# A transformer block on one core: reordering the products of the first 2048 projection columns

## The chip, the cores and the metric

The kernel runs on one core of one Trainium2 chip. The core has a matrix engine (TensorE: its matmuls are PE in the profile, its weight loads PEld), VectorE (DVE), ScalarE (ACT), GpSimd (POOL) and SyncE (SP), which issues most of the DMA transfers here. The metric is the device time of one execution in microseconds. Before the change it is 437.45 us as the median of three executions (437.12 to 437.57).

## The reference

The program computes one block: modulation of the input by vectors made from a condition c, a token mixer (attention and retention heads), a normalisation, and a feed-forward part. What this case touches is the beginning:

```python
mod = jax.nn.silu(c) @ w_ada[l] + b_ada[l]
sh1, sc1, g1, sh2, sc2, g2 = jnp.split(mod[:, None, :], N_MOD, axis=-1)
h = x * (1.0 + sc1) + sh1          # 256 tokens x 1024
...
proj = h @ w_in                    # the first 2048 columns: mq, mk, mv, rq
```

All inputs are float32. Every large product is made from three products of rounded parts: each operand is split into a high part (float32 rounded to the format the matmul takes, `F32R`) and a low part (the operand less its high part). The result is high x high + high x low + low x high, summed in PSUM.

## The kernel before

Weights go from HBM into `raw` tiles (128 x 2048 float32, 1 MB, four buffers), issued by SP in `load_raw` (L74). For each half of a raw tile, ScalarE makes the high part `whi` (L66) and VectorE the low part `wlo` (L67); later in the kernel the same pair stands in L1028 and L1042. TensorE then multiplies.

The first stage, "A", makes `h @ w_in[:, :2048]`. The contraction of 1024 is cut in eight k-tiles j of 128. The result (256 tokens x 2048 columns) fills all eight PSUM banks: bank `half * 4 + c * 2 + t` holds token half t and 512 columns. So each k-tile has 8 banks x 3 products = 24 matmuls of 128 x 512, with the tokens as the stationary operand.

Before the products of k-tile j, its part of h must exist. An ada tile holds 128 columns of w_ada for the scale and 128 for the shift, transposed, with 1024 elements each. VectorE multiplies these by the row silu(c) and sums them (`ada`, L154, with a read of the accumulator each), and adds the bias column (L171). Then h is formed from x by scale and bias: `hh`, its high part (named A in the profile, L176 on ScalarE; for j = 0 on VectorE, L189), `h32`, the same in full float32 (A7a or A7b, L176 on ScalarE), and `hl` = h32 - hh (L178 on VectorE).

The order of the work is written out by hand in `SEQ`: "a0 W0 P0 a1 W1 P1 a2 W2 P2 a3 W3 P3 X0 Q0 a4 X1 W4 Q1 P4 a5 W5 P5 ...". "a" sums an ada tile, "W" splits a k-tile's weights and makes its h, "P" issues its products. "X" and "Q" are two weight tiles of another projection (winX), whose products reuse banks 0 to 3 after k-tile 3: after P3 ScalarE copies banks 0 to 3 out (L241), four matmuls with zeros open the banks anew (L218), and the winX products follow (mm3, L81 to L83, 128 x 256). There is no scheduler: each engine runs its instructions in the order in which the program issues them.

Each consumed raw tile lets `load_A` issue the next load, in the order of SEQ: ada tile, then x of the k-tile (L120, tile A3a, A3b, A6a or A6b) and its weights. `PIECES` says into how many transfers a load is cut. Transfers on SP use eight semaphores in turn, so that one waits for the eighth before it to have landed.

At the very start SP loads `first` (c, an identity and biases), then ada tile 0 in pieces of 512, 512 and 1024 columns, then x and the weights of k-tile 0 in four pieces of 512 columns, and then the tiles of k-tile 1. Three float32 matmuls on the first piece (L149) keep TensorE busy until k-tile 0's products.

In `products_A`, k-tiles 0 and 1 (`j < CHUNK`, L204) issue for each 512 columns hh x hi, hh x lo and hl x hi, two matmuls each. From k-tile 2 on, each bank gets its three products one behind the other through `mm3` (L81 hh x hi, L82 hh x lo, L83 hl x hi).

Of the kernel before, what the change touches and what calls it, by code (L numbers as in the profile page):

```python
# [9 lines left out]
AF = mybir.ActivationFunctionType  # L10
OP = mybir.AluOpType
# [16 lines left out]
CONST_AT, FIRST = 1, 2  # L28
T0_AT, XN, PRIME = 4, 256, 3
W0, W1, W2 = (4, 5), (6,), (7,)  # L30
PIECES = dict(ada1=[(0, 512, 1024, 2048)] + [2] * 3 + [1] * 4, winA=[4] * 2 + [2] * 2 + [1] * 4, winX=[1] * 2)
CHUNK = 2
BUSY = 3
SEQ = [(s[0], int(s[1])) for s in
# [17 lines left out]
def _body(nc, a, out, pe, act, dve, sp, cst, wts, big, tmp, ps, dram):  # L52
    f = lambda ap: ap.bitcast(F32)

    def bank(i):
        return ps.tile([128, 512], F32, tag=f"P{i}", name=f"P{i}")

    def slot(n, shape, dt=F32):
        return big.tile(shape, dt, tag=f"A{n}", name=f"A{n}")
# [5 lines left out]
    def split(hi, lo, src):  # L65
        act.activation(hi, src, AF.Copy)  # L66
        dve.tensor_tensor(lo, src, f(hi), OP.subtract)  # L67


    def load_raw(src, pieces=1):  # L70
        t = wts.tile([128, 2048], F32, tag="raw", name="raw", bufs=RAW_BUFS)
        cuts = range(0, 2049, 2048 // pieces) if isinstance(pieces, int) else pieces
        for c0, c1 in zip(cuts, cuts[1:]):
            sp.dma_start(t[:, c0:c1], src[:, c0:c1])  # L74
        return t

    def new_hl():
        return [wts.tile([128, 1024], F32R, tag=n, name=n, bufs=HL_BUFS) for n in ("whi", "wlo")]

    def mm3(o, lh, ll, rh, rl, start, stop):  # L80
        pe.matmul(o, lh, rh, start=start, stop=False)  # L81
        pe.matmul(o, lh, rl, start=False, stop=False)  # L82
        pe.matmul(o, ll, rh, start=False, stop=stop)  # L83
# [67 lines left out]
    def ada(raw, sec, j, rows=slice(0, 1024)):  # L151

        junk = tmp.tile([128, 1024], mybir.dt.bfloat16, name="junk", bufs=1)
        dve.tensor_tensor_reduce(out=junk[:, rows], in0=raw[:, rows], in1=srow[:, rows], scale=1.0, scalar=0.0,  # L154
                                 op0=OP.mult, op1=OP.add, accum_out=mod[:, sec, j:j + 1])


    hh = slot(0, [128, 8, 256], F32R)
    hl = slot(1, [128, 8, 256], F32R)
    pa = [bank(i) for i in range(8)]  # L160

    def h1(j, part):

        if part == 0:
            ra = raws.pop(("ada1", j))
            if j == 0:
                ada(ra, 0, 0, slice(0, 512))
                dve.tensor_tensor(bcol[:, 0, 0:1], bcol[:, 0, 0:1], mod[:, 0, 0:1], OP.add)
            for i in range(2):
                ada(ra[:, i * 1024:(i + 1) * 1024], i, j, slice(512 if i == j == 0 else 0, 1024))  # L170
            dve.tensor_tensor(mod[:, 0:2, j], mod[:, 0:2, j], bcol[:, 0:2, j], OP.add)  # L171
            load_A()
        else:
            h32 = slot(("7a", "7b")[j % 2], [128, 256])
            for o in (h32,) if j == 0 else (hh[:, j], h32):
                act.activation(o, raws["xT", j], AF.Identity, scale=mod[:, 0, j:j + 1], bias=mod[:, 1, j:j + 1])  # L176
            raws.pop(("xT", j))
            dve.tensor_tensor(hl[:, j], h32, f(hh[:, j]), OP.subtract)  # L178

    def halves_A(name, j, mid=lambda: None):  # L180
        rw = raws.pop((name, j))
        for half in range(2):
            hi, lo = whl[name, j, half] = new_hl()
            w = 512 if name == "winA" and j < CHUNK else 1024
            mid_at = 512 if 0 < j < CHUNK else 0
            for c in range(0, 1024, w):
                if name == "winA" and j == half == c == 0:

                    dve.tensor_scalar(hh[:, 0], raws["xT", 0], mod[:, 0, 0:1], mod[:, 1, 0:1],  # L189
                                      op0=OP.mult, op1=OP.add)  # L190
                split(hi[:, c:c + w], lo[:, c:c + w], rw[:, half * 1024 + c:half * 1024 + c + w])
                if half == 0 and c == mid_at:
                    mid()
        load_A()

    def products_A(j):
        for half in range(2):
            hi, lo = whl.pop(("winA", j, half))
            for c in range(2):
                if j < CHUNK:  # L200
                    cs = slice(c * 512, (c + 1) * 512)
                    for i, (x, w) in enumerate(((hh, hi), (hh, lo), (hl, hi))):
                        for t in range(2):
                            pe.matmul(pa[half * 4 + c * 2 + t], x[:, j, t * 128:(t + 1) * 128], w[:, cs],  # L204
                                      start=i == j == 0, stop=False)
                    continue
                for t in range(2):
                    mm3(pa[half * 4 + c * 2 + t], hh[:, j, t * 128:(t + 1) * 128],
                        hl[:, j, t * 128:(t + 1) * 128], hi[:, c * 512:(c + 1) * 512],
                        lo[:, c * 512:(c + 1) * 512], j == 0 or j == 4 and half == 0,  # L210
                        j == 7 or j == 3 and half == 0)

    def products_X(u):

# [12 lines left out]
    whl = {}  # L227
    qk = [slot(n, [128, 1024]) for n in ("2a", "2b")]
    ga = slot(12, [128, 8, 256])
    for do, j in SEQ:  # L230
        if do == "a":
            h1(j, 0)
        elif do == "W":
            halves_A("winA", j, lambda: h1(j, 1))
        elif do == "X":
            halves_A("winX", j)
        elif do == "P":
            products_A(j)
            if j == 3:
                for i in range(4):  # L240
                    act.activation(qk[i % 2][:, i // 2 * 512:i // 2 * 512 + 512], pa[i], AF.Copy)  # L241
# [944 lines left out]
```

## Time and profile before

| | us |
|---|---|
| median of three executions | 437.45 |
| the profiled execution, its own time | 437.32 |
| its span in the trace | 435.5 |
| TensorE matmul busy | 422.5 (97%) |
| VectorE busy | 346.1 (79%) |
| ScalarE busy | 241.7 (55%) |

The granted TensorE clock of the profiled execution is 0.997 of full speed. Times in the rows are microseconds from the start of the span, durations as well unless marked ns. A row of the time line has start, duration, engine, line of the program, operation, what it writes and reads, and in brackets how long the engine was idle before it and what ended that. A matmul's duration covers its way through the pipeline: two matmuls that follow each other at full pace start closer together than their durations.

### The profile page before, as it was taken

How to read it: one execution, taken by the hardware profiler on the slowest of the kernel's cores; microseconds unless marked ns; L12 is line 12 of the kernel's file. 1: busy time of each engine (PE TensorE's matmuls, PEld its weight loads, DVE VectorE, ACT ScalarE, POOL GpSimd, SP SyncE). 2: the span in 40 equal slices, each digit the busy share in tenths (PEclk: the TensorE clock that was granted, in tenths of full speed). 3: DMA queues.
4: the chain of work that ended last, by engine and by line, in shares of the span. 5: the costliest groups of instructions: out<-in, count | busy, mean ns of one | idle time of the engine just before them, and what ended most of it. 6: DMA issues, size and time to landing. Idle time of an engine off the chain costs nothing.

```text
span 435.5 us, 6921 instructions
## 1 busy us (share of the span) xinstructions
PE 422.5 (97%) x2738; PEld 379.0 (87%) x2738; DVE 346.1 (79%) x550; ACT 241.7 (55%) x369; POOL 6.7 (2%) x16
## 2 busy tenths in 40 slices
PE   5999999999999999999999999999999999999993
PEld 2768888877788999999989899899999999999882
DVE  4979689979997999697779887798886665577476
ACT  4466578579774477543453995655445545355500
POOL 0000000100000000000000010000000000000000
PEclk9999999999999999999999999999999999999998
DMA  8999887787468778779672079577766784550001
GB/s 263 412 423 355 319 322 292 304 339 250 147 275 299 289 288 298 279 286 316 236 267 108 0 255 401 186 267 257 278 238 251 288 274 160 195 193 2 2 24 72
DMA packets 19696, 105.72 MB, mean 243 GB/s; under 512 B 2512, under 2 KB 4560, under 8 KB 8784
## 3 DMA queue, kind: packets, MB, share of 16 engines
q1 hardware_dynamic: 18288, 100.29, 62.1%
q0 software_dynamic: 1376, 4.99, 3.4%
q8 instruction: 21, 0.34, 0.3%
q14 instruction: 11, 0.09, 0.1%
HBM read 104.22 MB, written 1.06 MB: 242 GB/s over the span
## 4 chain that ended last, share of the span: by engine, by line
PE 92%; DMA 4%; DVE 2%; issue 1%; ACT 0%; SPq 0%; DVEq 0%
PE P L81 28%; PE P L82 28%; PE P L83 28%; DMA raw<-in_strm 3%; DMA A3b<-in_strm 1%; PE P L532 1%; PE P L534 1%; PE P L535 1%; PE P L776 1%; PE P L828 1%; PE P L847 1%; PE P L871 1%; DVE junk L154 1%; DVE wlo L67 0%; PE P L917 0%
## 5 line engine op out<-in xcount | busy, mean ns | idle before, releaser
L1042 DVE TENSOR_TENSOR wlo<-raw,whi 128x1024 fp32r<-128x1024 f32 x118 | 140.4, 1219 | 24.7 <-ACT whi L1028 24.7
L1028 ACT ACTIVATE whi<-raw 128x1024 fp32r<-128x1024 f32 x118 | 120.2, 1051 | 41.3 <-PE P L83 12.4
L83 PE MATMUL P<-whi,A 128*128 128x512 f32 (+1 forms) x212 | 80.3, 379 | 0.0
L81 PE MATMUL P<-whi,A 128*128 128x512 f32 (+1 forms) x168 | 65.4, 389 | 0.1
L82 PE MATMUL P<-wlo,A 128*128 128x512 f32 (+1 forms) x168 | 64.0, 381 | 0.5 <-DVE wlo L67 0.5
L154 DVE CUSTOM_DVE_ANT_0 junk<-raw,srow 128x1024 bf16<-128x1024 f32 (+1 forms) x49 | 58.7, 1197 | 3.5 <-ACT srow L141 1.8
L81 PE MATMUL P<-A3a,whi 128*128 128x256 f32 x192 | 54.4, 283 | 0.0
L81 PE MATMUL P<-A3b,whi 128*128 128x256 f32 x192 | 54.3, 283 | 0.0
L82 PE MATMUL P<-A6b,whi 128*128 128x256 f32 x192 | 54.3, 283 | 0.0
L83 PE MATMUL P<-A3b,wlo 128*128 128x256 f32 x192 | 54.3, 283 | 0.0
L83 PE MATMUL P<-A3a,wlo 128*128 128x256 f32 x192 | 54.3, 283 | 0.0
L82 PE MATMUL P<-A6a,whi 128*128 128x256 f32 x192 | 54.3, 283 | 0.0
L83 PEld LDWEIGHTS P<-whi,A 128*128 128x128 f32 x212 | 39.9, 188 | 7.9
L81 PE MATMUL P<-A,whi 128*128 128x256 f32 x160 | 45.9, 287 | 0.0
L83 PE MATMUL P<-A,wlo 128*128 128x256 f32 x160 | 45.2, 283 | 0.0
L82 PE MATMUL P<-A,whi 128*128 128x256 f32 x160 | 45.2, 283 | 0.0
L81 PEld LDWEIGHTS P<-whi,A 128*128 128x128 f32 x168 | 31.6, 188 | 7.1 <-issue 1.3
L82 PEld LDWEIGHTS P<-wlo,A 128*128 128x128 f32 x168 | 31.7, 188 | 6.7 <-DVE wlo L67 1.2
L82 PEld LDWEIGHTS P<-A6a,whi 128*128 128x128 f32 x192 | 36.8, 192 | 0.3
L81 PEld LDWEIGHTS P<-A3a,whi 128*128 128x128 f32 x192 | 36.8, 192 | 0.3
L81 PEld LDWEIGHTS P<-A3b,whi 128*128 128x128 f32 x192 | 36.9, 192 | 0.0
L82 PEld LDWEIGHTS P<-A6b,whi 128*128 128x128 f32 x192 | 36.9, 192 | 0.0
(235 smaller groups left out, 734.0 us busy)
## 6 DMA issues: line engine op xcount, KB each, us to landing
raw<-in_ada SPq DMA_DIRECT2D x16, 1024.0 KB, 5.2
raw<-in_wup SPq DMA_DIRECT2D x11, 1024.0 KB, 4.8
raw<-in_wgate SPq DMA_DIRECT2D x11, 1024.0 KB, 5.1
raw<-in_wdown SPq DMA_DIRECT2D x11, 1024.0 KB, 4.9
raw<-in_winB SPq DMA_DIRECT2D x10, 1024.0 KB, 5.8
raw<-in_strm SPq DMA_DIRECT2D x8, 1024.0 KB, 6.6
raw<-in_strm SPq DMA_DIRECT2D x11, 512.0 KB, 7.2
raw<-in_winGr SPq DMA_DIRECT2D x4, 1024.0 KB, 6.0
```

The lines of the kernel that those rows point to most:

```text
L81: pe.matmul(o, lh, rh, start=start, stop=False)
L82: pe.matmul(o, lh, rl, start=False, stop=False)
L83: pe.matmul(o, ll, rh, start=False, stop=stop)
L154: dve.tensor_tensor_reduce(out=junk[:, rows], in0=raw[:, rows], in1=srow[:, rows], scale=1.0, scalar=0.0, op0=OP.mult, op1=OP.add, accum_o ...
L532: pe.matmul(p, xl(k)[:, tk], hi[:, c], start=False, stop=k == 7)
L534: pe.matmul(p, xh(k)[:, tk], hi[:, c], start=k == 0, stop=False)
L535: pe.matmul(p, xh(k)[:, tk], lo[:, c], start=False, stop=False)
L776: pe.transpose(p[:, i * 128:(i + 1) * 128], roped[:, which * 512 + i * 128:which * 512 + (i + 1) * 128], ident)
L828: pe.matmul(ps2[e][:, c], qkT[0][s, h // 2, qb * 128:(qb + 1) * 128], qkT[1][s, h // 2, :128 + 128 * qb], start=True, stop=True)
L847: pe.matmul(p[64 * e:64 * e + 64, o], v[:, kb, 64 * (h + e):64 * (h + e) + 64], pT[e][:, c], start=kb == 0, stop=kb == 1)
L1028: act.activation(hi, src, AF.Copy)
L1042: dve.tensor_tensor(lo, src, f(hi), OP.subtract)
```

## The change

Three things are changed, all in stage A.

1. Ada tile 0 is loaded in four pieces of 512 columns (before: 512, 512, 1024). Its sums are made in four steps of 512, scale first, then shift; each first half is added into the bias column by a 128 x 1 add.
2. `h1` has three parts instead of two. Part 1 makes hh alone. It stands ahead of the first `whi` of a k-tile for j = 0 (on VectorE), and behind the first `whi` for the others (for j = 1 behind the first 512 columns; before, behind 1024). Part 2 makes h32 and hl, and stands behind the splits of half 1; for j = 3 and 7 behind those of half 0.
3. `products_A` issues, within a k-tile, all products of hh with both halves of the weights (hi, then lo, per 512 columns for j < 2 and per 1024 for the others), and then all products of hl with hi. For j = 3 and 7 this order is kept within half 0 and then within half 1.

The number of matmuls, of splits and of h activations stays the same. Ada tile 0 takes one more DMA, one more sum with its accumulator read, and one more 128 x 1 add.

```diff
-PIECES = dict(ada1=[(0, 512, 1024, 2048)] + [2] * 3 + [1] * 4, ...
+PIECES = dict(ada1=[4] + [2] * 3 + [1] * 4, ...
...
         if part == 0:
             ra = raws.pop(("ada1", j))
-            if j == 0:
-                ada(ra, 0, 0, slice(0, 512))
-                dve.tensor_tensor(bcol[:, 0, 0:1], bcol[:, 0, 0:1], mod[:, 0, 0:1], OP.add)
             for i in range(2):
-                ada(ra[:, i * 1024:(i + 1) * 1024], i, j, slice(512 if i == j == 0 else 0, 1024))
+                rw, at = ra[:, i * 1024:(i + 1) * 1024], 0 if j else 512
+                if at:
+                    ada(rw, i, j, slice(0, at))
+                    dve.tensor_tensor(bcol[:, i, j:j + 1], bcol[:, i, j:j + 1], mod[:, i, j:j + 1], OP.add)
+                ada(rw, i, j, slice(at, 1024))
             dve.tensor_tensor(mod[:, 0:2, j], mod[:, 0:2, j], bcol[:, 0:2, j], OP.add)
             load_A()
+        elif part == 1:
+            x, m = raws["xT", j], [mod[:, i, j:j + 1] for i in range(2)]
+            if j == 0:
+                dve.tensor_scalar(hh[:, j], x, *m, op0=OP.mult, op1=OP.add)
+            else:
+                act.activation(hh[:, j], x, AF.Identity, scale=m[0], bias=m[1])
         else:
             h32 = slot(("7a", "7b")[j % 2], [128, 256])
-            for o in (h32,) if j == 0 else (hh[:, j], h32):
-                act.activation(o, raws["xT", j], AF.Identity, scale=mod[:, 0, j:j + 1], bias=mod[:, 1, j:j + 1])
-            raws.pop(("xT", j))
+            act.activation(h32, raws.pop(("xT", j)), AF.Identity, scale=mod[:, 0, j:j + 1],
+                           bias=mod[:, 1, j:j + 1])
             dve.tensor_tensor(hl[:, j], h32, f(hh[:, j]), OP.subtract)
...
-            mid_at = 512 if 0 < j < CHUNK else 0
             for c in range(0, 1024, w):
-                if name == "winA" and j == half == c == 0:
-                    dve.tensor_scalar(hh[:, 0], raws["xT", 0], mod[:, 0, 0:1], mod[:, 1, 0:1],
-                                      op0=OP.mult, op1=OP.add)
+                first_ = name == "winA" and half == c == 0
+                if first_ and j == 0:
+                    h1(j, 1)
                 split(hi[:, c:c + w], lo[:, c:c + w], rw[:, half * 1024 + c:half * 1024 + c + w])
-                if half == 0 and c == mid_at:
-                    mid()
+                if first_ and j:
+                    h1(j, 1)
+            if name == "winA" and half == (j % 4 != 3):
+                h1(j, 2)
         load_A()

     def products_A(j):
...
+        ws = [whl.pop(("winA", j, half)) for half in range(2)]
+        parts = [(x, ks, (half,)) for half in range(2) for x, ks in ((hh, 2), (hl, 1))]
+        if j % 4 != 3:
+            parts = [(hh, 2, (0, 1)), (hl, 1, (0, 1))]
+        for x, ks, halves_ in parts:
+            for half in halves_:
+                w = 512 if j < CHUNK else 1024
+                for c0 in range(0, 1024, w):
+                    for k in range(ks):
+                        for c in range(c0, c0 + w, 512):
+                            for t in range(2):
+                                pe.matmul(pa[half * 4 + c // 512 * 2 + t], x[:, j, t * 128:(t + 1) * 128],
+                                          ws[half][k][:, c:c + 512],
+                                          start=ks == 2 and k == 0 and (j == 0 or j == 4 and half == 0),
+                                          stop=ks == 1 and (j == 7 or j == 3 and half == 0))
```

More of the change, by code (lines that the diff above doesn't have):

```diff
@@ L30 @@
 W0, W1, W2 = (4, 5), (6,), (7,)
-PIECES = dict(ada1=[(0, 512, 1024, 2048)] + [2] * 3 + [1] * 4, winA=[4] * 2 + [2] * 2 + [1] * 4, winX=[1] * 2)
+PIECES = dict(ada1=[4] + [2] * 3 + [1] * 4, winA=[4] * 2 + [2] * 2 + [1] * 4, winX=[1] * 2)
 CHUNK = 2
@@ L191, in halves_A @@
                 split(hi[:, c:c + w], lo[:, c:c + w], rw[:, half * 1024 + c:half * 1024 + c + w])
-                if half == 0 and c == mid_at:
-                    mid()
+                if first_ and j:
+                    h1(j, 1)
+            if name == "winA" and half == (j % 4 != 3):
+                h1(j, 2)
         load_A()
     def products_A(j):
[L197 to L211, printed above, removed]
@@ L233, in _body @@
         elif do == "W":
-            halves_A("winA", j, lambda: h1(j, 1))
+            halves_A("winA", j)
         elif do == "X":
```

2 lines of the change are left out of this document (1 added, 1 removed).

## The prediction

> **What bounds the kernel now.** I read the page first (its busy table and its chain), then the waits of TensorE, then the early part of the time line.
>
> ```profile
> span 435.5 us, 6921 instructions
> PE 422.5 (97%) x2738; PEld 379.0 (87%) x2738; DVE 346.1 (79%) x550; ACT 241.7 (55%) x369; POOL 6.7 (2%) x16
> PE 92%; DMA 4%; DVE 2%; issue 1%; ACT 0%; SPq 0%; DVEq 0%
> ```
>
> TensorE is busy 97% of the span and makes 92% of the chain that ended last. The change removes no product. So it can only win time in which TensorE waits, and these are the waits of its two streams (matmul and weight load) that bear on this change (view of the waits: us in total, times, longest):
>
> ```profile
> PE P L204 <- DVE A L189: 1.1, 1, 1.1
> PE P L82 <- DVE wlo L67: 0.5, 2, 0.3
> PE P L204 <- ACT A L176: 0.5, 1, 0.5
> PEld P L82 <- DVE wlo L67: 1.2, 2, 0.7
> ```
>
> All lie in the first 30 us. The matmul waits look small because a matmul that has been issued counts as busy until its pipeline is empty, so I measure losses by start times instead. Time line, TensorE, matmuls of k-tiles 2 and 3 and the first ones of X0 (start, duration, instruction):
>
> ```profile
> 22.20 0.50 PE L81 MATMUL P<-whi,A 128*128 128x512 f32 x1
> 22.97 0.51 PE L82 MATMUL P<-wlo,A 128*128 128x512 f32 x1 [0.27 <-DVE wlo L67]
> 23.32 0.50 PE L83 MATMUL P<-whi,A 128*128 128x512 f32 x1
> 23.65 0.39 PE L81 MATMUL P<-whi,A 128*128 128x512 f32 x1
> ...
> 28.43 0.39 PE L81 MATMUL P<-whi,A 128*128 128x512 f32 x1
> 29.06 0.50 PE L82 MATMUL P<-wlo,A 128*128 128x512 f32 x1 [0.24 <-DVE wlo L67]
> 29.73 0.39 PE L81 MATMUL P<-whi,A 128*128 128x512 f32 x1
> ...
> 35.57 0.39 PE L81 MATMUL P<-A,whi 128*128 128x256 f32 x1
> 35.91 0.27 PE L83 MATMUL P<-A,wlo 128*128 128x256 f32 x1
> ```
>
> K-tile 2 starts at 22.20, its fourth matmul at 23.65, and k-tile 3 (21 matmuls on) at 28.43: (28.43 - 23.65) / 21 = 0.228 us is the undisturbed pace. The first three matmuls took 1.45 us where three at pace take 0.68, because the second matmul needs the weights' low half, which comes last. K-tile 3 repeats it: 28.43 to 29.73 is 1.30. After a stall two matmuls come 0.33 to 0.35 apart before the pace is back (22.97, 23.32, 23.65); I call this the restart, 0.2 us in all. From 35.57 on (X0) no wait of a product is in the list.
>
> **What holds the start of k-tile 2.** ScalarE's rows, and one window row (its last two numbers are the DMA share and GB/s):
>
> ```profile
> 20.60 1.06 ACT L66 ACTIVATE whi<-raw 128x1024 fp32r<-128x1024 f32 x1 [2.75 <-DMA raw<-in_strm]
> 21.57 0.58 ACT L176 ACTIVATE A<-A6a,mod 128x256 fp32r<-128x256 f32 x1
> 22.06 0.59 ACT L176 ACTIVATE A7a<-A6a,mod 128x256 f32<-128x256 f32 x1
> 22.55 1.04 ACT L66 ACTIVATE whi<-raw 128x1024 fp32r<-128x1024 f32 x1
> 27.50 0.60 ACT L176 ACTIVATE A<-A6b,mod 128x256 fp32r<-128x256 f32 x1 [0.50 <-DVE mod L171]
> 29.93 0.60 ACT L241 ACTIVATE A2a<-P 128x512 f32<-128x512 f32 x1 [0.39 <-PE P L83]
> 32.49 2.00 ACT L66 ACTIVATE whi<-raw 128x1024 fp32r<-128x1024 f32 x2
> ```
> ```profile
> 10.00:20.00 10.00, 9.42 (x40) 7.26 (x41) 9.50 (x18) 5.00 (x10) 0.00 (x0) 1.00 1.04 412
> ```
>
> ScalarE waited 2.75 us for k-tile 2's first half of weights, which landed at 20.6; the DMA engines were full (share 1.04, 412 GB/s) since 10 us. Then come 1.06 us of whi and 0.58 of hh, to 22.15, and TensorE starts at 22.20. The change keeps this order (first whi, then hh, for j > 0), so **k-tile 2 starts at 22.20 whatever was won before it**.
>
> **Part 1: the first ada tile in four pieces.** The start, VectorE (its last sum before h, and h itself) and TensorE's first product:
>
> ```profile
> 8.09 1.23 DVE L154 CUSTOM_DVE_ANT_0 junk<-raw,srow 128x1024 bf16<-128x1024 f32 x1 [1.40 <-DMA raw<-in_strm]
> 9.55 0.41 DVE L189 TENSOR_SCALAR A<-A3a,mod 128x256 fp32r<-128x256 f32 x1
> 10.11 0.47 PE L204 MATMUL P<-whi,A 128*128 128x512 f32 x1 [1.13 <-DVE A L189]
> ```
>
> VectorE idles 1.40 us until the 512 KB piece has landed and then sums 1024 columns in 1.23 us. With two pieces the first 512 fall into that idle time and half of 1.23 is left, so h and the first product come about 0.5 us earlier (one more read of the accumulator and one more 128x1 add lie in the idle time too). K-tiles 0 and 1 then start up to 0.5 us earlier, k-tile 1 also because its hh (ScalarE) no longer stands behind two whi pieces. All of it ends in a longer wait for the landing at 20.6. Value on the path: 0.
>
> The price is one more transfer on SP's queue. SP's issues of this tile's three pieces and of the fourth piece of the first weights, and then issue to landing of the first of the one and of the other (256 KB each):
>
> ```profile
> 1.17 1.37 SPq L74 DMA_DIRECT2D raw<-in_strm  x3
> 4.48 1.01 SPq L74 DMA_DIRECT2D raw<-in_strm  x1
> ```
> ```profile
> raw<-in_strm SPq DMA_DIRECT2D x1, 256.0 KB, 3.0
> raw<-in_strm SPq DMA_DIRECT2D x1, 256.0 KB, 6.4
> ```
>
> The later piece takes 6.4 where the first takes 3.0: everything after the start queues behind bytes, so SP's extra issue ((1.37 - 0.42) / 2 = 0.47 us) is covered by that backlog, and with it the loads of x and of the first weights that stand behind it on SP. Upper end: the whole latency of a piece in series, 3.0 less its own 0.64 us of data at 412 GB/s, 2.4 us. Lower end: the pieces run sooner and all landings come some tenths earlier. The same bytes go through full engines, which is nearest to no shift; I take +0.03.
>
> **Part 2: all products of hh first, then hl.** For k-tile 2 the order becomes four hi (0.9 us), four lo, the same for half 1, then eight of hl with hi. VectorE's rows for this stretch:
>
> ```profile
> 21.70 1.23 DVE L67 TENSOR_TENSOR wlo<-raw,whi 128x1024 fp32r<-128x1024 f32 x1 [0.43 <-ACT whi L66]
> 22.84 0.42 DVE L178 TENSOR_TENSOR A<-A7a,A 128x256 fp32r<-128x256 f32 x1
> 23.62 1.22 DVE L67 TENSOR_TENSOR wlo<-raw,whi 128x1024 fp32r<-128x1024 f32 x1 [0.37 <-ACT whi L66]
> 24.77 1.22 DVE L154 CUSTOM_DVE_ANT_0 junk<-raw,srow 128x1024 bf16<-128x1024 f32 x1
> 27.30 0.17 DVE L171 TENSOR_TENSOR mod<-mod,first 128x2 f32<-128x2 f32 x1
> 33.58 1.23 DVE L67 TENSOR_TENSOR wlo<-raw,whi 128x1024 fp32r<-128x1024 f32 x1 [2.78 <-ACT whi L66]
> ```
>
> The low half is ready at 21.70 + 1.23 = 22.93. The first lo product now comes at 22.20 + 0.2 + 4 x 0.228 = 23.3: no stall. ScalarE makes whi of half 1 at 22.06 instead of 22.55 (the h32 activation goes behind it), ready 23.1; its first use is at 24.2. VectorE's lo of half 1 then starts at 23.13 and ends near 24.35; first use 25.1. hl follows by 24.75; first use 26.0. K-tile 2 would end at 22.20 + 0.2 + 24 x 0.228 = 27.87 instead of 28.43.
>
> *What is late next*: k-tile 3's hh, which waits for its two ada sums. They start when VectorE is done with k-tile 2: before at 24.77; now lo at 23.13, next start 1.15 on (23.62 to 24.77), hl at 0.42 less the 0.09 by which VectorE's instructions overlap (22.93 against 22.84): 24.61. That is 0.16 earlier, less a few hundredths for the order of waits: I take 0.14. So mod is done at 27.33, hh runs 27.36 to 27.96, TensorE starts k-tile 3 at 28.00 instead of 28.43: **-0.43**. Inside it the low half (28.9 on VectorE) is needed only after four products, 28.00 + 0.2 + 0.91 = 29.1, and hl and the second half have more room still. The fourth matmul falls at 28.00 + 0.2 + 0.68 = 28.9 instead of 29.73, so a further **-0.40**; together -0.83 at X0, whose first matmul moves from 35.57 to 34.74.
>
> *Does X0 take it?* Its third matmul needs the low half made at 33.58 + 1.23 = 34.81, and would come at 35.91 - 0.83 = 35.08. That low half hangs on whi at 32.49, behind ScalarE's four copies of banks 0 to 3. Bank 0 is now full only after half 0's last product, at 30.4 (before: copy at 29.93). Before, the copies came as TensorE filled the banks; now all four banks are full within 0.7 us and ScalarE can run them at its own pace, 0.49 between two starts by 21.57 and 22.06 with 0.58 busy; at 0.52 they are through at 32.5, as before. Cover left: 0.27.
>
> *Further on* k-tiles 4 to 7 had no stall, so the order there is worth nothing. The smallest lead of a weights' low half after X0 that I find is
>
> ```profile
> 72.31 1.22 DVE L1042 TENSOR_TENSOR wlo<-raw,whi 128x1024 fp32r<-128x1024 f32 x1
> 74.63 0.39 PE L82 MATMUL P<-wlo,A 128*128 128x512 f32 x1
> ```
>
> ready at 73.53, used at 74.63: 1.10 us, more than 0.83. So the win should reach the end.
>
> **Sum.** -0.43 - 0.40 + 0.03 = -0.80 us. The profiled execution took 437.32 us (span 435.5 and 1.8 around it), 0.13 under the median of 437.45. So 436.52 for it and **436.65 as the median**. A change of 0.2% is 0.87 us and is about what a measurement of this kernel tells from no change; the forecast lies just inside it.
>
> **Rivals.**
> *(a) The landings come earlier* (the stream of the first 10 us runs better in four equal pieces). For: VectorE's 1.40 us wait shows the 512 KB piece late. Against: the same bytes. K-tile 2 could start earlier until its mod is the last to come, about 0.3 us before the whi that holds it now. Gain 1.1: 436.35.
> *(b) The copies of banks 0 to 3 are slower than I assume.* For: they now start later, at 30.4. Against: every ScalarE pair above starts 0.49 apart. At 0.69 per copy whi of X0 starts at 33.2, its low half is ready at 35.5, X0's third matmul at 35.6, and the gain is 0.3: 437.15.
> *(c) The other side: the fourth piece delays the whole stream.* All landings up to k-tile 2 come in one order through full engines, so a delay at the head is kept. At the upper end of 2.4 us: -0.80 + 2.4 = +1.6, 439.05. It is slower by more than 0.2% only if k-tile 2's landing comes 1.7 us later, at 22.3. Against it speaks the 6.4 us backlog above, in which a fixed latency is hidden.
> [...]
> *(d) It does nothing*, because TensorE's start of k-tile 2 is DMA-held and k-tile 3's is held by hh: this is right for the starts, but the stalls behind the starts (1.45 and 1.30 us for three matmuls) are plain in the rows.
>
> **How the numbers follow.** Forecast 0.63, own range 436.4 to 436.95; (a) 0.12; (b) and smaller losses like it, (d) among them, 0.17; (c) 0.08. The range 436.2 to 437.3 holds all but (c) and the ends. Faster by over 0.2% (under 436.58) are (a) and somewhat over a third of the forecast's range: 0.36. Slower is (c): 0.08. The rest, 0.56, is within.
>
> **What would show it.** Right: TensorE's first product near 9.65; ScalarE's whi of k-tile 2 still at about 20.6 and the start at 22.2; from there an even 0.228 us pace with no wait for wlo; k-tile 3 at 28.0 after a short wait for hh; X0 near 34.75. Wrong: whi of k-tile 2 at another time than 20.6 by more than 0.3; X0's third matmul waiting for wlo; a new wait between 66 and 80 us, where VectorE is nearly full.

## The result, and the profile after

The changed kernel took 435.8 us as the median of seven executions, the kernel before 437.4 us beside it. The ratio is 0.9968 with a 95% interval of 0.9956 to 0.9979, that is 1.4 us less (0.9 to 1.9). In a second comparison on another chip it was 0.9975 (0.9967 to 0.9984). The forecast of 436.65 us is too high, and the time lies below its range.

The profiled execution of the changed kernel took 436.03 us. From its page the span, the busy table and the chain that ended last:

```profile
span 434.3 us, 6926 instructions
PE 422.7 (97%) x2738; PEld 379.0 (87%) x2738; DVE 346.5 (80%) x553; ACT 240.9 (55%) x369; POOL 6.7 (2%) x16
PE 89%; DMA 5%; DVE 2%; SPq 1%; issue 1%; ACT 1%; DVEq 0%; ACTq 0%
```

The matmuls are the same 2738, with nearly the same busy time (422.5 us before, 422.7 after); what was won is waiting. The last product of the kernel before, and then that of the changed kernel, in the time lines of TensorE:

```profile
427.68 0.28 PE L83 MATMUL P<-whi,A 128*128 128x256 f32 x1
```
```profile
426.48 0.28 PE L83 MATMUL P<-whi,A 128*128 128x256 f32 x1
```

It comes 1.20 us earlier. Where does that arise? TensorE in stage A of the changed kernel (start, us from the first start to the last end of a group, instruction, how many):

```profile
9.08 0.70 PE L216 MATMUL P<-whi,A 128*128 128x512 f32 x2
...
15.16 0.73 PE L216 MATMUL P<-whi,A 128*128 128x512 f32 x2 [0.29 <-ACT A L180]
...
21.32 1.21 PE L216 MATMUL P<-whi,A 128*128 128x512 f32 x4 [0.42 <-ACT A L180]
22.36 1.09 PE L216 MATMUL P<-wlo,A 128*128 128x512 f32 x4
...
28.14 1.07 PE L216 MATMUL P<-wlo,A 128*128 128x512 f32 x4
...
33.73 0.39 PE L81 MATMUL P<-A,whi 128*128 128x256 f32 x1
33.96 0.28 PE L82 MATMUL P<-A,whi 128*128 128x256 f32 x1
34.07 0.27 PE L83 MATMUL P<-A,wlo 128*128 128x256 f32 x1
...
45.34 1.35 PE L216 MATMUL P<-whi,A 128*128 128x512 f32 x4
...
47.45 1.07 PE L216 MATMUL P<-whi,A 128*128 128x512 f32 x4
```

The first product moved from 10.11 to 9.08, the start of k-tile 2 from 22.20 to 21.32, and X0 from 35.57 to 33.73. So 1.84 us are won by X0: 0.88 of it is already there when k-tile 2 starts, and 0.96 comes inside k-tiles 2 and 3. After X0 some is given back: the first eight products of k-tile 4 take 47.45 - 45.34 = 2.11 us where eight at the pace of 0.228 take 1.82. ScalarE shows both the gain and the loss:

```profile
19.71 1.06 ACT L66 ACTIVATE whi<-raw 128x1024 fp32r<-128x1024 f32 x1 [2.55 <-DMA raw<-in_strm]
20.68 0.58 ACT L180 ACTIVATE A<-A6a,mod 128x256 fp32r<-128x256 f32 x1
...
26.45 0.60 ACT L180 ACTIVATE A<-A6b,mod 128x256 fp32r<-128x256 f32 x1 [0.36 <-DVE mod L172]
...
29.48 0.60 ACT L249 ACTIVATE A2a<-P 128x512 f32<-128x512 f32 x1 [0.98 <-PE P L216]
29.97 0.59 ACT L249 ACTIVATE A2b<-P 128x512 f32<-128x512 f32 x1
...
31.40 2.02 ACT L66 ACTIVATE whi<-raw 128x1024 fp32r<-128x1024 f32 x2
...
43.38 2.76 ACT L254 ACTIVATE A<-P 128x512 f32<-128x512 f32 x4 [3.11 <-PE P L83]
...
79.58 1.06 ACT L1036 ACTIVATE whi<-raw 128x1024 fp32r<-128x1024 f32 x1 [3.97 <-DMA raw<-in_winB]
```

K-tile 2's first weights landed at 19.71 instead of 20.60. K-tile 3's hh still waits for its sums, and ends at 26.45 + 0.60 = 27.05. The four copies of the winX result (L254) take 2.76 us, 0.69 each, from 43.38; k-tile 4's first four products need all four banks and cannot be through before 46.1. That is the new stall.

The list of waits of TensorE's weight loads says the same:

```profile
PEld P L216 <- ACT A L180: 2.0, 3, 0.8
PEld P L784 <- ACT A3a L786: 0.5, 1, 0.5
PEld P L216 <- ACT A L254: 0.4, 1, 0.4
```

The third line is the stall at k-tile 4. The second is another loss, near 82 us: a late weight tile of another stage held ScalarE for 3.97 us (the last row above), and copies of PSUM behind it. TensorE's lead over the kernel before is 1.56 us ahead of this place (79.85 and 78.29) and 1.20 behind it (84.25 and 83.05). So with 0.27 and 0.36 us given back, the 1.84 of X0 become the 1.20 at the end. In the second profile of this kernel that wait is missing, and the lead falls only from 1.61 at X0 to 1.34 at the end.

### The profile page after: what moved, and what is told of

The parts are those of the page before. It is cut to its first block, busy times and chain, and to the rows that moved or that the text cites. A ratio compares the mean times of both kernels' runs of the same rounds, so it can differ in the third digit from the quotient of the medians.

```text
span 434.3 us, 6926 instructions
## 1 busy us (share of the span) xinstructions
PE 422.7 (97%) x2738; PEld 379.0 (87%) x2738; DVE 346.5 (80%) x553; ACT 240.9 (55%) x369; POOL 6.7 (2%) x16
## 4 chain that ended last, share of the span: by engine, by line
PE 89%; DMA 5%; DVE 2%; SPq 1%; issue 1%; ACT 1%; DVEq 0%; ACTq 0%
PE P L81 25%; PE P L83 25%; PE P L82 24%; PE P L216 7%; DMA raw<-in_strm 3%; DMA raw<-in_winB 2%; SPq L74 1%; PE P L540 1%; PE P L542 1%; PE P L543 1%; PE P L836 1%; PE P L855 1%; PE P L879 1%; PE P L784 1%; DVE wlo L1050 1%
## 5 line engine op out<-in xcount | busy, mean ns | idle before, releaser
L83 PE MATMUL P<-whi,A 128*128 128x512 f32 (+1 forms) x164 | 61.4, 375 | 0.0
L81 PE MATMUL P<-whi,A 128*128 128x512 f32 (+1 forms) x120 | 46.6, 388 | 0.0
L82 PE MATMUL P<-wlo,A 128*128 128x512 f32 (+1 forms) x120 | 45.0, 375 | 0.0
L83 PEld LDWEIGHTS P<-A3b,wlo 128*128 128x128 f32 x192 | 36.9, 192 | 0.0
L83 PEld LDWEIGHTS P<-A3a,wlo 128*128 128x128 f32 x192 | 36.8, 192 | 0.0
L83 PEld LDWEIGHTS P<-whi,A 128*128 128x128 f32 x164 | 30.9, 188 | 5.7
```

## The experiments

What had to be explained: the start of k-tile 2 moved by 0.88 us, and the prediction had said that it would not move. Two theories were set against each other first. One (letter L): the four pieces make the landings earlier. The other (letter B where the expectations use letters): the new order frees buffers earlier, so that later loads are issued earlier, and the pieces do nothing. No kernel below leaves out any part of the computation. In this table "ratio" is the time over that of the kernel before on the same chip; "rate" is the last number of the row of the stretch from 4 to 8 us; "weights" is the start of ScalarE's first split of k-tile 2, that is the landing.

| kernel | ada tile 0 in columns | median us | ratio (95%) | rate GB/s | weights |
|---|---|---|---|---|---|
| before | 512, 512, 1024 | | 1 | 299 | 20.60 |
| changed | 4 x 512 | 435.8 | 0.9968 (0.9956 to 0.9979) | 352 | 19.71 |
| changed, again | 4 x 512 | 435.82 | 0.9975 (0.9967 to 0.9984) | 328 | 19.89 |
| order_only | 512, 512, 1024 | 436.28 | 0.9984 (0.9975 to 0.9993) | 304 | 19.95 |
| pieces_only | 4 x 512 | 436.34 | 0.9981 (0.9972 to 0.9990) | 357 | 19.24 |
| big_piece | 512, 512, 1024 | 436.75 | 0.9994 (0.9985 to 1.0003) | 292 | 20.28 |
| bank_order_4 | 4 x 512 | 435.51 | 0.9968 (0.9956 to 0.9981) | 336 | 19.90 |
| bank_order_again | 4 x 512 | 435.64 | 0.9969 (0.9959 to 0.9978) | 338 | 20.09 |
| two_in_four | 4 x 512 | 435.78 | 0.9971 (0.9961 to 0.9981) | 356 | 20.05 |
| long_rows | 512, 512, 2 x 64 rows of 1024 | 436.90 | 1.0003 (0.9994 to 1.0012) | 233 | 21.11 |
| two_halves | 1024, 1024 | 435.80 | 0.9974 (0.9966 to 0.9983) | 384 | 18.91 |
| eight | 8 x 256 | 438.22 | 1.0029 (1.0019 to 1.0038) | 245 | 21.96 |
| long_first | 1024, 512, 512 | 435.95 | 0.9967 (0.9955 to 0.9980) | 379 | 19.39 |
| three_alike | 704, 704, 640 | 435.55 | 0.9960 (0.9946 to 0.9974) | 373 | 19.70 |
| plain_halves | 1024, 1024 | 435.35 | 0.9954 (0.9941 to 0.9966) | 375 | 19.36 |
| plain_again | 1024, 1024 | 435.39 | 0.9963 (0.9949 to 0.9977) | 378 | 19.66 |
| busy_one | 1024, 1024 | 435.58 | 0.9969 (0.9958 to 0.9979) | 374 | 19.46 |

The medians come from several chips, so compare the ratios. Rate and landing are those of one execution each. Kernels with the same loads differ in the landing by up to 0.85 us (19.24 to 20.09 with four pieces, 19.95 to 20.60 with the old cut), and the two groups overlap, so the ratios decide; a row shows where time can lie, not what a kernel gains in the mean.

### Order alone, pieces alone

The changed kernel with the loads and sums of ada tile 0 as before:

```diff
-PIECES = dict(ada1=[4] + [2] * 3 + [1] * 4, ...
+PIECES = dict(ada1=[(0, 512, 1024, 2048)] + [2] * 3 + [1] * 4, ...
...
+            if j == 0:
+                ada(ra, 0, 0, slice(0, 512))
+                dve.tensor_tensor(bcol[:, 0, 0:1], bcol[:, 0, 0:1], mod[:, 0, 0:1], OP.add)
             for i in range(2):
-                rw, at = ra[:, i * 1024:(i + 1) * 1024], 0 if j else 512
-                if at:
-                    ada(rw, i, j, slice(0, at))
-                    dve.tensor_tensor(bcol[:, i, j:j + 1], bcol[:, i, j:j + 1], mod[:, i, j:j + 1], OP.add)
-                ada(rw, i, j, slice(at, 1024))
+                ada(ra[:, i * 1024:(i + 1) * 1024], i, j, slice(512 if i == j == 0 else 0, 1024))
```

> The new order of products and of hh, h32 and hl, but ada tile 0 loaded and summed as before (512, 512, 1024 columns). Theory L (the 512 KB piece with 4 KB rows is what makes all early landings late): ScalarE's whi of k-tile 2 stays at 20.6, k-tile 3 starts at 28.0, X0 near 34.75, and the time is 0.7 to 0.9 us below before. Theory B (the new order frees buffers sooner, and so the loads come sooner): whi of k-tile 2 comes at 19.7 here too, X0 near 33.7, and the time is that of the changed kernel, 1.4 to 1.6 below before.

The kernel before with the four pieces and the four sums, in the old order of the products:

```diff
-PIECES = dict(ada1=[(0, 512, 1024, 2048)] + [2] * 3 + [1] * 4, ...
+PIECES = dict(ada1=[4] + [2] * 3 + [1] * 4, ...
...
-            if j == 0:
-                ada(ra, 0, 0, slice(0, 512))
-                dve.tensor_tensor(bcol[:, 0, 0:1], bcol[:, 0, 0:1], mod[:, 0, 0:1], OP.add)
             for i in range(2):
-                ada(ra[:, i * 1024:(i + 1) * 1024], i, j, slice(512 if i == j == 0 else 0, 1024))
+                rw, at = ra[:, i * 1024:(i + 1) * 1024], 0 if j else 512
+                if at:
+                    ada(rw, i, j, slice(0, at))
+                    dve.tensor_tensor(bcol[:, i, j:j + 1], bcol[:, i, j:j + 1], mod[:, i, j:j + 1], OP.add)
+                ada(rw, i, j, slice(at, 1024))
```

> Before, with ada tile 0 loaded in four pieces and summed in four steps; all products and h in the old order. Theory L: whi of k-tile 2 at 19.7, the stalls behind the first products of k-tiles 2 and 3 stay (1.45 and 1.30 us for three matmuls), X0 near 34.7, time 0.7 to 0.9 us below before. Theory B: whi of k-tile 2 at 20.6, X0 at 35.6, no change of time beyond 0.1 us.

With the kernel before at 437.15 us on that chip, the order alone is worth 437.15 x (1 - 0.9984) = 0.70 us (0.3 to 1.1) and the pieces alone 0.83 us (0.4 to 1.2). Their sum, 1.5, is near what the whole change gave (1.4, and 1.1 in its second comparison). So the two parts are about equal, adding up lies within the intervals, and the pieces are not worth nothing. Order alone, in TensorE's time line and ScalarE's:

```profile
21.55 1.20 PE L215 MATMUL P<-whi,A 128*128 128x512 f32 x4 [0.40 <-ACT A L179]
22.59 1.08 PE L215 MATMUL P<-wlo,A 128*128 128x512 f32 x4
...
34.01 0.39 PE L81 MATMUL P<-A,whi 128*128 128x256 f32 x1
```
```profile
19.95 1.06 ACT L66 ACTIVATE whi<-raw 128x1024 fp32r<-128x1024 f32 x1 [2.53 <-DMA raw<-in_strm]
20.92 0.58 ACT L179 ACTIVATE A<-A6a,mod 128x256 fp32r<-128x256 f32 x1
```

and pieces alone, TensorE, ScalarE and the stretch from 4 to 8 us (columns: the stretch, its length, busy time of PE, PEld, DVE, ACT and POOL, granted clock, DMA share, GB/s):

```profile
20.85 0.50 PE L81 MATMUL P<-whi,A 128*128 128x512 f32 x1
...
33.92 0.39 PE L81 MATMUL P<-A,whi 128*128 128x256 f32 x1
```
```profile
19.24 1.06 ACT L66 ACTIVATE whi<-raw 128x1024 fp32r<-128x1024 f32 x1 [2.73 <-DMA raw<-in_strm]
```
```profile
4.00:8.00 4.00, 3.88 (x11) 1.83 (x10) 2.81 (x9) 1.51 (x3) 0.00 (x0) 1.00 1.01 357
```

The same stretch of the kernel before:

```profile
4.00:8.00 4.00, 3.88 (x11) 1.72 (x10) 1.56 (x5) 1.20 (x2) 0.00 (x0) 1.00 0.89 299
```

From the start of k-tile 2 to X0 the kernel before took 35.57 - 22.20 = 13.37 us, order alone takes 34.01 - 21.55 = 12.46 and pieces alone 33.92 - 20.85 = 13.07. So the order works inside k-tiles 2 and 3 (0.91 us), and the pieces mainly work ahead of them.

The landing is less tidy. With order alone it came at 19.95, not at the 20.6 of the first theory, and X0 at 34.01, not at 34.75; only the time was as that theory had it. But these 0.65 us cannot come from the order. They are there when the third piece of ada tile 0 lands, where the two kernels have run the same instructions so far: VectorE's sum of it starts at 8.09 before (the row in the prediction) and with order alone at

```profile
7.42 1.22 DVE L154 CUSTOM_DVE_ANT_0 junk<-raw,srow 128x1024 bf16<-128x1024 f32 x1 [0.83 <-DMA raw<-in_strm]
```

So 0.67 us lie between two executions of the same start. The load of x for k-tile 1 (A3b) is the eighth transfer behind the last piece of ada tile 0, and SP issues it when that piece has landed: before, with order alone, and with pieces alone at

```profile
7.97 0.33 SPq L120 DMA_DIRECT2D A3b<-in_strm  x1
```
```profile
7.30 0.33 SPq L120 DMA_DIRECT2D A3b<-in_strm  x1
```
```profile
6.49 0.33 SPq L120 DMA_DIRECT2D A3b<-in_strm  x1
```

Here the two cuts do not overlap: 7.30 to 7.97 in the three kernels with 512, 512, 1024, and 6.48 to 6.98 in the five with four pieces and all else loaded alike. From there on a delay is passed on: in all seventeen profiles ScalarE's first split of k-tile 2 starts 7.0 to 7.1 us after SP has issued x of k-tile 2 (20.60 - 13.55 before, 19.71 - 12.70 in the changed kernel).

Pieces alone give 357 GB/s in the stretch from 4 to 8 us instead of 299, with the order as before, so theory B falls: the pieces do something without the order. The same bytes run sooner. (357 - 299) GB/s x 4 us are 232 KB, which at 412 GB/s is 0.56 us. That is of the size of the 0.83 us that the pieces alone are worth, but less than half of the 1.36 us by which the landing came earlier in this profile. This execution was the fastest of its eleven (435.60 us, the median is 436.34), so its landing overstates the gain, and the rate of the stretch is a sign of an early stream and not the whole account.

### Not the sums: the cut

Four sums with the old cut tells whether the sums or the transfers matter:

```diff
-PIECES = dict(ada1=[4] + [2] * 3 + [1] * 4, ...
+PIECES = dict(ada1=[(0, 512, 1024, 2048)] + [2] * 3 + [1] * 4, ...
```

> The changed kernel, its sums in four steps, but the last two of them on one DMA of 1024 columns (512 KB, 4 KB rows). Theory L: landings as before (whi of k-tile 2 at 20.6), X0 near 34.75, 0.7 to 0.9 us below before. If the four sums and not the DMA were the cause: whi at 19.7, as in the changed kernel.

It kept 0.26 us (1 - 0.9994 of 437.15) of the change's gain, with an interval that holds zero, and its rate was 292 GB/s. Four sums do not bring the gain back. They seem to cost some: 0.7 to 0.9 us were expected to stay, as with order alone. In its profile the last two sums stand behind the long piece, and hh of k-tile 2 waits 0.30 us for mod. At four sums in the new order, what counts is how the tile is cut into transfers: 0.9994 with the old cut, 0.9968 and 0.9975 with four pieces.

### The new stall, and more pieces

The changed kernel with the products of k-tiles 4 to 7 bank by bank, as before the change:

```diff
+        if j >= 4:
+            for half in range(2):
+                hi, lo = ws[half]
+                for c in range(2):
+                    for t in range(2):
+                        mm3(pa[half * 4 + c * 2 + t], hh[:, j, t * 128:(t + 1) * 128],
+                            hl[:, j, t * 128:(t + 1) * 128], hi[:, c * 512:(c + 1) * 512],
+                            lo[:, c * 512:(c + 1) * 512], j == 4 and half == 0, j == 7)
+            return
         for x, ks, halves_ in parts:
```

> The changed kernel, but k-tiles 4 to 7 issue their products bank by bank as before. In the changed kernel k-tile 4 asks for banks 0 to 3 within its first four matmuls, while ScalarE copies them out at 0.69 us each; its first eight matmuls lose 0.26 us. Expected: k-tile 4 runs at its pace from its first matmul, and a time 0.1 to 0.3 us below the changed kernel's; no difference if a later wait takes it back.

> The changed kernel once more, beside the next one on the same chip: 1.3 to 1.7 us below before.

> Products of k-tiles 4 to 7 bank by bank, all else as changed. If k-tile 4's 0.26 us reach the end, 0.2 to 0.3 us below the changed kernel; if a later wait takes them back, the same.

Here are the first and the ninth product of k-tile 4 with the products bank by bank:

```profile
45.52 0.40 PE L81 MATMUL P<-whi,A 128*128 128x512 f32 x1
...
47.36 0.39 PE L83 MATMUL P<-whi,A 128*128 128x512 f32 x1
```

The eight products between take 1.84 us instead of 2.11: bank by bank, TensorE asks for a new bank every three products (0.69 us), just the pace of the copies. The stall of 0.27 us is gone in the trace. The times do not settle the price: the ratios are 0.9968 beside 0.9968, and 0.9969 beside 0.9975 on one chip, where 0.9975 is 1.1 us below before (1.3 to 1.7 were expected). The intervals overlap: shown is the stall, not its price.

Would the second ada tile gain from four pieces too (with the bank order)? Letter R stands for long rows (of 4 KB) being slow at the start, letter S for the size or the number of the transfers deciding.

```diff
-PIECES = dict(ada1=[4] + [2] * 3 + [1] * 4, ...
+PIECES = dict(ada1=[4] * 2 + [2] * 2 + [1] * 4, ...
```

> As the kernel with products of k-tiles 4 to 7 bank by bank, and ada tile 1 in four pieces of 2 KB rows as well. Theory R: its landings come a little earlier too, whi of k-tile 2 0.2 to 0.4 us before 19.7 to 19.9, and the time falls by as much. Theory S: no change, or up to 0.1 us later.

It did not: 0.9971 beside 0.9969 without it.

### Which cut, and why

If not the number of sums, is it the long rows of the third piece (theory R; a row of 1024 columns is 4 KB, of 512 it is 2 KB)? Two transfers of 64 partitions keep four transfers of 256 KB each but give the second half of the tile long rows:

```diff
+        if pieces == 4 and not raws:
+            for c0, c1 in ((0, 512), (512, 1024)):
+                sp.dma_start(t[:, c0:c1], src[:, c0:c1])
+            for p0 in (0, 64):
+                sp.dma_start(t[p0:p0 + 64, 1024:], src[p0:p0 + 64, 1024:])
+            return t
```

> The changed kernel; the second half of ada tile 0 still comes as two transfers of 256 KB, but cut by partitions (64 x 1024 columns, 4 KB rows) in place of by columns (128 x 512, 2 KB rows). Theory R (long rows make the early transfers slow): these two land as late as the 512 KB piece did, the last of them near 7.3 to 7.9, and the time is 0.5 to 0.9 us above the changed kernel's. Theory S (the size of one transfer, or the number of transfers behind which it stands, decides): they land near 6.5 as in the changed kernel; the sums of columns must wait for both, which costs the start 0.3 us but not the start of k-tile 2, and the time stays within 0.2 us of the changed kernel's.

It took away all of the change's gain (1.0003), 436.90 us beside 435.82 for the changed kernel on the same chip, and gave the lowest rate of all, by this row:

```profile
4.00:8.00 4.00, 3.94 (x10) 1.80 (x8) 1.56 (x5) 1.19 (x2) 0.00 (x0) 1.00 0.90 233
```

So transfers of one size are not what matters, and long rows looked guilty (or the 64 partitions, which came in with them). The theory of long rows predicts that a tile in two transfers, with long rows only, is bad, and one in eight, with short rows only, is good:

```diff
-PIECES = dict(ada1=[4] + [2] * 3 + [1] * 4, ...
+PIECES = dict(ada1=[2] + [2] * 3 + [1] * 4, ...
```

> The changed kernel, ada tile 0 in two transfers of 1024 columns (512 KB, 4 KB rows each). Theory R (long rows are slow in the first 8 us, whatever the cut): the DMA rate between 4 and 8 us stays near 240 to 320 GB/s as with the other long pieces (four short pieces: 300 to 375), whi of k-tile 2 at 20.3 to 21.2, time 0.5 to 1.2 us above the changed kernel.

```diff
-PIECES = dict(ada1=[4] + [2] * 3 + [1] * 4, ...
+PIECES = dict(ada1=[8] + [2] * 3 + [1] * 4, ...
```

> The changed kernel, ada tile 0 in eight transfers of 256 columns (128 KB, 1 KB rows). Theory R, carried on: no slower landings than with 2 KB rows, whi of k-tile 2 at 19.5 to 20.0, time within 0.3 us of the changed kernel. If it is the bytes in flight that count (only eight transfers may be on their way, and these are small), the stream starves at the start and whi of k-tile 2 comes 0.5 us or more later.

For this theory both came out the other way. The stretch from 4 to 8 us with two halves:

```profile
4.00:8.00 4.00, 3.94 (x11) 2.18 (x10) 2.35 (x8) 1.76 (x3) 0.00 (x0) 1.00 1.02 384
```

That is the highest rate, with long rows only, so theory R falls. With eight pieces the kernel is slower than before (1.0029), with 245 GB/s. Its expectation had named another reason for a late landing, too few bytes in flight with eight transfers allowed. But up to 8.28 us SP issues without a pause: its rows end and start at 4.92 and 4.96, 5.39 and 5.44, 8.24 and 8.28, so none of these issues waited for a landing. SP's queue shows a limit of its own:

```profile
1.18 3.74 SPq L74 DMA_DIRECT2D raw<-in_strm  x8
```

Eight issues take 3.74 us, 0.47 each, and each carries only 128 KB: 128 KB in 0.47 us is 279 GB/s, less than the 412 at which the stream runs later. So the issues are the likely limit here; no run changed them alone. In two_halves the landing was the earliest of all (18.91) and yet the time was no better than with four pieces: VectorE still made four sums of 512, the first at 5.40 us, on a piece of 512 KB, where it came at 4.89 with four pieces, and hh of k-tile 2 then waited 0.89 us for mod.

Three theories were left: a mix of row lengths within the tile is bad (M); a cut into three is bad (C); or a step from short rows to longer ones, as the stream starts, is bad (F). A cut 1024, 512, 512 has the mix and the count, but steps down; 704, 704, 640 has the count without a step up. The third kernel is the simplest one that the results pointed to: two transfers, two plain sums of 1024 columns as for every other ada tile, and k-tiles 4 to 7 bank by bank.

```diff
-PIECES = dict(ada1=[4] + [2] * 3 + [1] * 4, ...
+PIECES = dict(ada1=[(0, 1024, 1536, 2048)] + [2] * 3 + [1] * 4, ...
```

> The changed kernel, ada tile 0 cut 1024, 512, 512. Theory M (a mix of row lengths at the start makes the stream slow): the whole tile has landed at 7.3 or later, as with 512, 512, 1024, the DMA rate between 4 and 8 us is 240 to 325 GB/s, the time 0.5 us or more above the changed kernel. Theory F (only the step from short rows to long ones is slow): the tile has landed by 6.5, rate 360 to 390, time within 0.3 us of the changed kernel.

```diff
-PIECES = dict(ada1=[4] + [2] * 3 + [1] * 4, ...
+PIECES = dict(ada1=[(0, 704, 1408, 2048)] + [2] * 3 + [1] * 4, ...
```

> The changed kernel, ada tile 0 cut 704, 704, 640: three transfers as before, but rows of nearly one length. Theories M and F: landed by 6.5, time within 0.3 us of the changed kernel. Theory C (it is the number of transfers, three and not two or four, that is unlucky): landed at 7.3 or later, time 0.5 us or more above it.

```diff
-PIECES = dict(ada1=[4] + [2] * 3 + [1] * 4, ...
+PIECES = dict(ada1=[2] * 4 + [1] * 4, ...
...
-                rw, at = ra[:, i * 1024:(i + 1) * 1024], 0 if j else 512
-                if at:
-                    ada(rw, i, j, slice(0, at))
-                    dve.tensor_tensor(bcol[:, i, j:j + 1], bcol[:, i, j:j + 1], mod[:, i, j:j + 1], OP.add)
-                ada(rw, i, j, slice(at, 1024))
+                ada(ra[:, i * 1024:(i + 1) * 1024], i, j)
```

> The new order for k-tiles 0 to 3, products of k-tiles 4 to 7 bank by bank, ada tile 0 in two transfers of 1024 columns and summed like the others, one sum of 1024 for the scale and one for the shift. With two halves and four sums the weights of k-tile 2 were there at 18.9, but hh of k-tile 2 waited for VectorE, whose sums ended at 8.84. Two sums of 1.23 take 0.7 us less than four of 0.69 with their reads and adds: the first product near 8.8, k-tile 2 at 20.8 to 21.0, X0 at 33.2 to 33.4, time 0.3 to 0.7 us below the changed kernel (435.1 to 435.5).

The rows of 1024, 512, 512 and then of 704, 704, 640:

```profile
4.00:8.00 4.00, 3.72 (x9) 1.75 (x8) 2.28 (x8) 1.56 (x3) 0.00 (x0) 1.00 1.03 379
```
```profile
4.00:8.00 4.00, 3.94 (x10) 1.74 (x8) 2.81 (x9) 1.19 (x2) 0.00 (x0) 1.00 1.03 373
```

Neither the mix nor the count of three is bad. What is left that fits is the step up: 512 columns first and 1024 behind them gave 233 to 304 GB/s in four kernels; every cut without a step up within the tile, eight pieces aside, gave 328 to 384. This is a rule found over seven cuts, with the rate of one execution for each kernel, and not a mechanism: what makes it so stays open. Plain halves had the lowest median of all runs, within the range that was expected, but not by the way expected: k-tile 2 started at about 21.7 us, not at 20.8 to 21.0, and X0 at 33.66.

### What holds the start now

In the profile of plain_halves TensorE's first product stood at 10.39, behind the three float32 matmuls (L149) that only keep TensorE busy: they wait for the first half of the tile (0.4 us in TensorE's list of waits). One instead of three:

```diff
-BUSY = 3
+BUSY = 1
```

> The kernel with two plain halves of ada tile 0, and one float32 warm-up matmul on its first piece instead of three (the warm-up products are thrown away; nothing of the computation is left out). In the run with three, TensorE's first product stands at 10.39 behind these matmuls, which wait for the first half of the tile to land (5.45); h is ready before that. Theory T (TensorE's start is now held by the warm-up matmuls, and this counts): first product near 9.0, k-tile 2 held by its landing or its hh near 20.9 instead of 21.72 by TensorE itself, X0 at 33.0 to 33.3 instead of 33.66, time 0.3 to 0.7 us under the run beside it. Theory L (the landing holds the start of k-tile 2 anyway, as in all runs before): first product near 9.0, k-tile 2 within 0.2 of 21.7, the same time within 0.2.

> The kernel with two plain halves of ada tile 0 and the products of k-tiles 4 to 7 bank by bank, once more, beside the run with one warm-up matmul. It was 0.9954 of the time before (0.9941 to 0.9966). Expected: 0.995 to 0.997; if it is over 0.997 its lead over the changed kernel was chance.

TensorE's first products, in the time line of the kernel with one:

```profile
9.04 0.70 PE L221 MATMUL P<-whi,A 128*128 128x512 f32 x2 [1.97 <-DVE A L174]
...
10.13 1.01 PE L221 MATMUL P<-whi,A 128*128 128x512 f32 x2
10.94 1.05 PE L221 MATMUL P<-wlo,A 128*128 128x512 f32 x2
11.79 1.05 PE L221 MATMUL P<-whi,A 128*128 128x512 f32 x2
```

The first product came at 9.04, as both theories had it, and nothing was won: 0.9969 beside 0.9963. From 10.94 on two products are 0.85 us apart where they are 0.46 at full pace. The stretches show why (the third number from the end is the granted clock):

```profile
10.00:11.00 1.00, 1.00 (x5) 0.76 (x4) 1.00 (x3) 0.96 (x2) 0.00 (x0) 0.58 1.01 397
11.00:13.00 2.00, 2.00 (x6) 1.59 (x5) 1.97 (x5) 0.00 (x0) 0.00 (x0) 0.50 1.04 396
13.00:14.00 1.00, 1.00 (x5) 0.75 (x3) 1.00 (x2) 0.63 (x1) 0.00 (x0) 0.72 1.03 397
```

The clock lost is 0.42 + 2 x 0.50 + 0.28 = 1.70 us, that is half rate for 3.4 us. It began about 1 us after a gap of 1.97 us without a matmul. In this execution the head start was spent on slow products. With three warm-up matmuls the clock was 1.00 in all these stretches. Neither theory had this: the landing theory was right on the time, but what held k-tile 2 here was TensorE itself, which came late out of k-tile 1 (its hh was ready at 20.42 + 0.59 = 21.01, the start was near 21.7).

That the slow products are why nothing was won is not shown. A loss of 1.70 us lowers the mean clock of an execution by 0.004. Four of the eight executions have a mean clock of 0.991 or 0.992, and took 435.38 to 435.53 us; the other four have 0.994 to 0.996, as with three warm-up matmuls, and took 435.62 to 436.52. So the executions without the loss were no faster.

Plain halves, measured again at 0.9963, is the fastest form found. Its products of k-tiles 4 to 7 go bank by bank, so the kernels to compare are bank_order_4 and bank_order_again (0.9968 and 0.9969 against 0.9954 and 0.9963); the intervals overlap, so that lead is likely and not shown. Its sums of ada tile 0 are also the shorter code.

## Why the prediction was wrong

**The step that failed** is part 1's "Value on the path: 0" with "+0.03" for the landings, and with it the bold sentence that k-tile 2 starts at 22.20 whatever was won before it. The pieces alone measured -0.83 us (0.4 to 1.2). The reading of the place was right: k-tile 2's start is held by a landing, and in the changed kernel too it is (ScalarE waited 2.55 us for it). The sign that the prediction itself set for being wrong, whi of k-tile 2 more than 0.3 us away from 20.6, is there: 19.71 and 19.89. The first product, forecast near 9.65, came at 9.08. Wrong was to take the landing as fixed because "the same bytes go through full engines". That was read from 10 to 20 us, where the rate was 412 GB/s. The bytes that the edit changes go earlier: from 4 to 8 us the kernel before moved 299 GB/s with a DMA share of 0.89. One more window row, at the place where the edit changes transfers, would have shown that there might be something to win: at 412 GB/s, (412 - 299) x 4 us are 0.45 MB, or 1.1 us. And one profile could not show where the landing lies to better than some tenths, as the 0.67 us between two executions of the same start tell. Why the old cut makes the start slow stays open. The lower bound ("all landings come some tenths earlier") was in the text and was not carried into the range.

**Part 2, the order, held in mechanism and nearly in size**: -0.83 was forecast at X0 and to the end. From k-tile 2's start to X0 the traces show -0.91 with the order alone (13.37 to 12.46) and -0.96 in the changed kernel (12.41); 0.27 of it is lost again at k-tile 4, and the order alone measured -0.70 (0.3 to 1.1). That -0.70 comes so near to -0.83 is in part luck: a somewhat larger gain and a loss that was not forecast. In the profile of the changed kernel k-tile 2's four hi products took 22.36 - 21.32 = 1.04 us before the first lo product, which did not wait; the forecast had 1.1. K-tile 3's start followed k-tile 2's by 27.11 - 21.32 = 5.8 us, as forecast (28.00 - 22.20), and was again held by hh behind mod, the thing that was named as late next: hh ended at 27.05. X0's third matmul came at 34.07 without waiting, and the copies of banks 0 to 3 ran 0.49 apart (29.48, 29.97), so rival (b) and rival (d) did not come true.

**"K-tiles 4 to 7 had no stall, so the order there is worth nothing"** was wrong by 0.27 us in the trace. A place without a stall can get one: the new order asks for four banks in the first four products, where the old asked for one bank in three. The prediction had asked this for the copies after k-tile 3 and not for those after the winX products, which run at 0.69.

**Rival (a)**, landings earlier, had the right direction at 0.12. Its time, 436.35, came from a cap, that mod would be next to hold at 0.3 us. But the sums for k-tile 2 stand on VectorE behind the work on the first tiles, and moved with it: that mod was done at 21.10 + 0.16 = 21.26 before and at 20.34 + 0.16 = 20.50 in the changed kernel. So the cap moved too.

**Rival (c)**, a fourth piece that delays the stream, did not come; with eight pieces it did, most likely from 0.47 us of SP per issue. The latency of a piece in series, 2.4 us in the prediction's upper end, is shown as a sum by no run: one piece more cost nothing (0.9981 with the pieces alone), and eight pieces instead of four cost (1.0029 - 0.9975) x 437 = 2.4 us in all, not 2.4 for each of the four.

## What to carry to other kernels

When an edit changes how something is loaded, read the rate of the transfers in the very stretch in which these loads run, not the average behind it: a start-up below the later rate (here 299 GB/s from 4 to 8 us and 412 from 10 to 20) may be time to win, even where the bytes stay the same. Measure the landing of the first pieces in more than one execution: here 0.67 us lay between two executions of the same start. In this kernel the stream started best with the first tile cut into two to four like transfers, or with the longer rows first (328 to 384 GB/s from 4 to 8 us); with eight pieces, at 0.47 us of the issuing queue each, it was 245. When products are reordered over PSUM banks, ask at each place where banks change hands how many banks the first products want, and at what pace they are copied out (here 0.49 us a bank at one place and 0.69 at another).

## What was not expected of the hardware

With a 512 KB transfer of 4 KB rows behind two of 2 KB rows the stream started slowly: 292 to 304 GB/s from 4 to 8 us, 233 with 4 KB rows over 64 partitions, against 328 to 357 for four pieces of 512 columns and 373 to 384 for cuts of 1024, 1024, of 1024, 512, 512 and of 704, 704, 640. Why is open.

With one warm-up matmul the granted clock of TensorE was 0.58 from 10 to 11 us, 0.50 from 11 to 13 and 0.72 from 13 to 14, which adds up to half rate for 3.4 us, and 1.00 from 14 to 16. The slow stretch began about 1 us after a gap of 1.97 us without a matmul. With three warm-up matmuls the clock was 1.00 in all these stretches. What starts such a stretch, and what ends it, no run shows.
